# A hybrid decoder block on one core: values split within their own heads, quarter sums in two passes, convolution steps at uneven gaps

## The chip, the cores and the metric

The kernel runs on one core of one Trainium2 chip. The metric is the device time of one execution in microseconds, as the median of several runs. A core has TensorE (PE in the profile, PEld for its weight loads), VectorE (DVE), ScalarE (ACT), GpSimd (POOL) and SyncE (SP), each with its own queue of instructions that it works through in order; they wait for each other through semaphores. In this kernel nearly all DMAs are issued by SP.

## What is computed

One decoder layer on 1024 tokens of width 1024, in float32:

```python
h = rms_norm(x, g_pre_mix);  z = h @ w_in
q, k, v, glu_in, z_ga, z_gc = split(z)
y_attn = dilated_attention_mixer(q, k, v, rel_bias_table, w_attn_out)
y_conv = conformer_conv_mixer(glu_in, ...)   # GLU, causal depthwise conv of 31 taps, layer norm, silu, w_conv_out
merged = sigmoid(z_ga) * y_attn + sigmoid(z_gc) * y_conv
x = x + rms_norm(merged @ w_mix_out, g_post_mix)
x = x + rms_norm(swiglu_ffn(rms_norm(x, g_pre_ffn), w_ffn_in, w_ffn_out), g_post_ffn)
```

The attention has three groups of eight heads (width 64) with dilations 1, 4 and 16; in each group a query sees a band of 128 tokens' span (in its residue class) with a T5 bias. The three groups' outputs are merged with weights from their softmax denominators.

## The kernel before

Every float32 product is made of three products of reduced-precision halves (fp32r): a tensor is split into hi (a cast on ScalarE) and lo (a subtraction, on VectorE or GpSimd), and TensorE adds hi·hi, hi·lo and lo·hi. Most large products save one in eight by a Strassen-Winograd scheme on 2x2 quarters, `winograd` (L308): seven products of quarters in the order A11·B11, A12·B21, S2·T2, S1·T1, S3·T3, S4·B22, A22·T4. The S are sums of weight quarters (`quarters`, L183, in six steps c = 0 to 5, their lo halves and sums on the engine `wsplit`); the T are sums of the activation's quarters, made once per stage by `quarter_sums` (L341) and kept split.

The program's order is written by hand. `tick` (L113) is called after every k-tile, that is after three matmuls of 512 columns; it steps every generator in `gens` (a generator that yields n rests n ticks) and runs what is due: loads and weight splits, and one piece of weight splitting every `PIECE` ticks. `beat` (L131) is called after every matmul of the V products and of some later ones and steps the attention's generator at a rate of 0.33 or 0.66 per matmul. A product of `winograd` has four ticks, a pair of output tiles 28.

The stages:

1. `start` and the first GLU tiles, without the scheme, while the activation is normalised.
2. For GLU tile 3 (`FIRST` = 4) the quarter sums run as a generator: for each of four quarter tiles, T1 = b11 - b12, T2 = b22 - T1 (sign turned), T3 = b22 - b12 on `wsplit` (GpSimd here), T4, and their splits. `B.finish(qs)` (in `build`) issues what is left of them; then the convolution's generator joins.
3. 23 pairs with the scheme: 4 of GLU, 4 and 3 of gates, 12 of q and k (`qk_pair`, L735). An eviction adds the bank to a copied half on VectorE (L677, L682, L686, L710, L720; for q and k L761, L764, L771, L777, L783). Beside them `conv` (L595) does the depthwise convolution on VectorE: for each of 8 channel tiles, even and odd phases and their sum (L620), then 16 rounds of up to three multiply-adds into PSUM (L637, L632, L634), 47 steps, with a gap of 0 or 1 tick behind each (`CONV`), then the recombination (L642 to L647) and a running sum on GpSimd (L653).
4. The V products (`v`, L843) beside `conv_norm` (L1059) and then `attention` (L882). The attention has 12 pairs of heads of 8 steps. At step s: scores on TensorE (L937) and the bias with a running minimum on VectorE (L940) for block s; exponentials on ScalarE (L950) for s - 1; transposes (L973) and the split of the probabilities (L978 on ScalarE, L979 on VectorE) for s - 3; the product with V (L994, L996) for s - 4, reduced by VectorE (L1001). `stacks` (L790) loads q, k and the bias of the next pair at the present pair's second step and has GpSimd copy q to the other 64 partitions (L806, L807). `values` (L820) loads V at the fifth step, `value_parts` (L834) splits it at the seventh and eighth: a cast on ScalarE (L839), a subtraction on GpSimd (L840). The attention starts when `conv_norm` is done. In the third group `others` (L811) loads the two other groups' outputs and statistics, and `merge` (L1010) combines the three: small operations on the statistics (L1018 to L1025), three products with weights (L1029, the first on GpSimd), two sums (L1031, L1033) and transposes (L1040 to L1044).
5. The last gate tiles and the convolution's output projection, beside the attention's rest (`conv_split`, L1051, L1052; evictions L1348); the attention's output projection; the mix projection with its norm (L1409).
6. The FFN: two plain tile pairs, quarter sums again, 20 tiles with the scheme, and the output projection in seven products over 11 weight pairs (L1673).

Activations that are made early and used late go through DRAM (`d_u`, `d_conv`, `d_qk`, `d_v`, `d_att`, `d_st`). SBUF has 44 slots of 128 x 1024 ("b" in the profile) and 13 halves ("c"). PSUM has 8 banks, divided anew for some stages by `banks`; a division starts with the tag that is asked for first.

## Time and profile before

| | |
|---|---|
| median of 3 runs | 1788.83 us (1788.06 to 1788.92) |
| the profiled execution's own time | 1787.76 us |
| its span, first to last instruction | 1786.0 us |
| TensorE busy | 1725.8 us (97%), mean granted clock 0.986 |
| VectorE busy | 1251.7 us (70%) |
| ScalarE busy | 790.9 us (44%) |
| GpSimd busy | 505.8 us (28%) |
| moved by DMA | 274.94 MB, mean 154 GB/s |

A profile is of one execution. Times in it are us from the first instruction. A row of the table of waits reads: engine, tile and line that waited, the engine and line that it waited for, us in total, times, longest. A row by stretches reads: the stretch, its length, and for PE, PEld, DVE, ACT and POOL the busy us with the number of instructions in brackets; then the granted clock of TensorE, the DMA engines' busy share and GB/s. A row of groups reads: line, engine, operation, output and inputs by tile name, shape, count, then busy us and the mean in ns, then the idle time before and its causes. In a timeline a row has start, duration and the instruction, and in brackets the idle time before it and what ended it. A busy PE includes matmuls at a halved clock.

### The profile page before, as it was taken

To read this page: it belongs to the slowest core of one execution; us is meant where nothing else is said; L and a number is where in the kernel's file an instruction comes from. 1 tells how busy PE (TensorE), PEld (TensorE's weight loads), DVE (VectorE), ACT (ScalarE), POOL (GpSimd) and SP (SyncE) were. 2 spreads that over 40 slices of the span, in tenths; PEclk is the share of its full clock that TensorE was granted. 3 is DMA by queue.
4 is the path that set the end of the run, shared out by engine and by line. 5 is a ranking of instruction groups with operands and counts; after the bars stand their busy time and mean duration, and the time that the engine had idled before them with its cause. 6 is when DMAs were issued, how large, how long until landed. Compare 5 with 4: busy or idle time off the path is not lost.

```text
span 1786.0 us, 24511 instructions
## 1 busy us (share of the span) xinstructions
PE 1725.8 (97%) x8698; PEld 1462.3 (82%) x8698; DVE 1251.7 (70%) x2198; ACT 790.9 (44%) x1549; POOL 505.8 (28%) x357
## 2 busy tenths in 40 slices
PE   8989999999999989999898999999999999999998
PEld 6768888887777989998687888888888888878886
DVE  6899867899996546555676475586566565567686
ACT  6344344334433456556553145653333333353453
POOL 0067777877773223332320040040000000000000
PEclk9999999999999989999889999999999999999999
DMA  4333334556667576667753753203223223395234
GB/s 159 140 118 123 119 118 147 154 165 174 186 165 224 161 215 181 190 186 232 264 182 104 261 193 107 100 36 123 89 89 140 90 89 124 130 333 170 95 134 148
DMA packets 185783, 274.94 MB, mean 154 GB/s; under 512 B 56113, under 2 KB 107948, under 8 KB 185660
## 3 DMA queue, kind: packets, MB, share of 16 engines
q1 hardware_dynamic: 185020, 272.74, 47.6%
q8 instruction: 68, 1.11, 0.3%
q10 hardware_dynamic: 576, 0.56, 0.1%
q14 instruction: 55, 0.45, 0.1%
q0 software_dynamic: 64, 0.07, 0.0%
HBM read 183.76 MB, written 94.28 MB: 156 GB/s over the span
## 4 chain that ended last, share of the span: by engine, by line
PE 64%; DVE 5%; DMA 3%; ACT 2%; issue 1%; POOL 0%; SPq 0%; DVEq 0%; ACTq 0%; POOLq 0%
PE p L1673 12%; PE p L305 8%; PE p L303 8%; PE p L304 8%; PE p L1409 5%; PE p L291 3%; PE p L289 3%; PE p L287 3%; PE p L865 3%; PE p L867 3%; PE p L863 2%; PE p L937 2%; PE p L973 1%; PE p L996 1%; DMA b<-dv 1%
## 5 line engine op out<-in xcount | busy, mean ns | idle before, releaser
L303 PE MATMUL p<-b,b 128*128 128x512 f32 x1204 | 471.1, 391 | 14.0 <-DVE c L777 7.3
L305 PE MATMUL p<-b,b 128*128 128x512 f32 x1204 | 470.1, 390 | 0.4 <-POOL b L180 0.4
L304 PE MATMUL p<-b,b 128*128 128x512 f32 x1204 | 470.0, 390 | 0.0
L303 PEld LDWEIGHTS p<-b,b 128*128 128x128 f32 x1204 | 226.9, 188 | 64.8 <-DVE c L777 9.2
L305 PEld LDWEIGHTS p<-b,b 128*128 128x128 f32 x1204 | 227.0, 189 | 48.9 <-POOL b L180 1.5
L304 PEld LDWEIGHTS p<-b,b 128*128 128x128 f32 x1204 | 226.9, 188 | 46.7
L179 ACT CAST b<-b 128x1024 fp32r<-128x1024 f32 x129 | 135.6, 1051 | 181.0 <-POOL b L200 71.0
L1673 PE MATMUL p<-b,b 128*128 128x512 f32 x924 | 209.7, 389 | 1.5 <-DVE c L1582 1.5
L180 POOL TENSOR_TENSOR b<-b,b 128x1024 fp32r<-128x1024 f32 x72 | 175.6, 2438 | 115.7 <-ACT b L179 99.7
L1673 PEld LDWEIGHTS p<-b,b 128*128 128x128 f32 x924 | 173.3, 188 | 37.9 <-DVE c L1582 1.9
L637 DVE SCALAR_TENSOR_TENSOR p<-b,par,p 128x511 f32<-128x511 f32 (+14 forms) x232 | 163.6, 738 | 0.0
L180 DVE TENSOR_TENSOR b<-b,b 128x1024 fp32r<-128x1024 f32 x57 | 69.7, 1223 | 123.8 <-ACT b L179 123.8
L287 PE MATMUL p<-b,b 128*128 128x512 f32 x368 | 152.7, 415 | 0.8 <-DVE b L1348 0.8
L291 PE MATMUL p<-b,b 128*128 128x512 f32 x368 | 150.9, 410 | 0.0
L289 PE MATMUL p<-b,b 128*128 128x512 f32 x368 | 150.5, 409 | 0.0
L1052 DVE TENSOR_TENSOR b<-c,b 128x512 fp32r<-128x512 f32 x125 | 90.7, 736 | 39.7 <-ACT b L1051 39.4
L863 PE MATMUL p<-b,b 128*128 128x256 f32 x384 | 114.7, 299 | 2.2 <-DVE c L783 2.2
L865 PE MATMUL p<-b,b 128*128 128x256 f32 x384 | 114.7, 299 | 0.9 <-DVE b L173 0.9
L867 PE MATMUL p<-b,b 128*128 128x256 f32 x384 | 114.0, 297 | 0.0
L1051 ACT CAST b<-c 128x512 fp32r<-128x512 f32 x125 | 76.5, 618 | 56.0 <-DVE c L355 17.6
L979 DVE TENSOR_TENSOR c<-p,c 128x256 fp32r<-128x256 f32 (+1 forms) x96 | 52.3, 545 | 68.5 <-ACT c L978 60.2
L1409 PE MATMUL p<-b,b 128*128 128x512 f32 x384 | 88.9, 391 | 0.0
(222 smaller groups left out, 3042.6 us busy)
## 6 DMA issues: line engine op xcount, KB each, us to landing
b<-w_in SPq DMA_DIRECT2D x53, 512.0 KB, 4.8
b<-w_fi SPq DMA_DIRECT2D x44, 512.0 KB, 4.8
dk<-c SPq DMA_DIRECT2D x96, 128.0 KB, 2.5
dq<-c SPq DMA_DIRECT2D x96, 128.0 KB, 2.4
b<-dq SPq DMA_DIRECT2D x48, 256.0 KB, 7.1
b<-dk SPq DMA_DIRECT2D x24, 512.0 KB, 8.5
dqS<-c SPq DMA_DIRECT2D x44, 256.0 KB, 2.2
b<-w_fo SPq DMA_DIRECT2D x44, 256.0 KB, 5.4
```

The lines of the kernel that those rows point to most:

```text
L180: self.wsplit.tensor_tensor(lo, x, f(hi), op=OP.subtract)
L287: nc.tensor.matmul(ps, hi[:, s], a, start=kt == 0, stop=False)
L289: nc.tensor.matmul(ps, hi[:, s], b, start=False, stop=False)
L291: nc.tensor.matmul(ps, lo[:, s], a, start=False, stop=kt == nk - 1)
L303: nc.tensor.matmul(ps, hi[:, s], a, start=first and kt == 0, stop=False, skip_group_check=True)
L304: nc.tensor.matmul(ps, hi[:, s], b, start=False, stop=False, skip_group_check=True)
L305: nc.tensor.matmul(ps, lo[:, s], a, start=False, stop=kt == 3, skip_group_check=True)
L637: nc.vector.scalar_tensor_tensor(A[i][:, j:], src[i][:, :H - j], w[i], A[i][:, j:], op0=OP.mult, op1=OP.add)
L865: nc.tensor.matmul(o, a, lo[:, s], start=False, stop=False)
L867: nc.tensor.matmul(o, b, hi[:, s], start=False, stop=kt == KT - 1)
L1409: nc.tensor.matmul(banks[tt][nh], st, wt[:, nh * H:(nh + 1) * H], start=bool(kt == 0 and a), stop=bool(kt == KT - 1 and b))
L1673: nc.tensor.matmul(acc[t], x, y, start=first and e == 0, stop=last and e == 2, skip_group_check=True)
```

## The change

Five things are changed together.

- **Quarter sums.** `quarter_sums` makes T1 and T2 of all four tiles in a first pass, writing T2 over b11, and then hands out `self.T`; T3 and T4 follow in a second pass, in place over b22 and b21. In stage 2 `first_sums` only makes sure of the first pass; the rest runs on beside the first pair and is finished behind its fourth product (S1), where `summed` then sets `wsplit` to GpSimd and lets the convolution join. Until there `wsplit` is VectorE.
- **Convolution.** The gaps behind a step are (0, 1, 0, 0, 0, 1) in turn, and (1, 1, 0, 1) from q and k on, in place of (0, 1, 0, 1, 0, 1, 1). The sum of the phases moves to GpSimd and is issued at round 14 of the tile before.
- **Values and copies.** V is loaded as soon as the split of the present pair's is issued, and split at the third and fourth step of its own pair. The copies of q (`double`) are issued behind the sixth and seventh step of the pair before. The twelve empty steps behind a late load go.
- **Merge.** The statistics' loads are issued at the sixth step (`other_stats`), the outputs' loads one step later than before. The merge starts with two further ticks' rest, all three weighted products are on VectorE, and there are two more ticks before the transposes.
- **Banks.** For the V stage and for the output projection one bank of another tag is asked for first, so that the tags lie on other banks.

```diff
@@ Build
+    T, sums = None, None
+
+    def first_sums(self, e):
+        while self.T is None:
+            next(e[0])
+        self.sums = e
@@ winograd, behind S1's product
         nc.scalar.copy(v1, V)
+        if self.sums:
+            self.finish(self.sums)
+            self.sums = None
+            self.summed()
@@ quarter_sums
+        T["B11"], T["B21"], T["B22"] = blocks
...
+        for i in range(4):
+            b11, b12, b22 = B[0][i], B[1][i], B[1][i + 4]
+            t1 = self.half()
+            nc.vector.tensor_tensor(t1, b11, b12, op=OP.subtract)
+            nc.vector.scalar_tensor_tensor(b11, t1, -1.0, b22, op0=OP.mult, op1=OP.subtract)
+            keep("T1", t1)
+            yield 1
+            keep("T2", b11)
+            yield 3
+        self.T = T
         for i in range(4):
             b11, b12, b21, b22 = B[0][i], B[1][i], B[0][i + 4], B[1][i + 4]
-            t1, t2, t3 = self.half(), self.half(), self.half()
-            nc.vector.tensor_tensor(t1, b11, b12, op=OP.subtract)
-            nc.vector.scalar_tensor_tensor(t2, t1, -1.0, b22, op0=OP.mult, op1=OP.subtract)
-            if last is not None:
-                keep("T4", last)
-                last = None
-            self.wsplit.tensor_tensor(t3, b22, b12, op=OP.subtract)
-            keep("T1", t1)
+            self.wsplit.tensor_tensor(b22, b22, b12, op=OP.subtract)
+            nc.vector.scalar_tensor_tensor(b21, b11, -1.0, b21, op0=OP.mult, op1=OP.subtract)
+            yield 0
+            keep("T3", b22)
             yield 1
-            nc.vector.scalar_tensor_tensor(t1, t2, -1.0, b21, op0=OP.mult, op1=OP.subtract)
-            keep("T2", t2)
-            keep("T3", t3)
...
-            yield 4
+            keep("T4", b21)
+            yield 0
@@ conv
+        def phases(u):
+            x = u.rearrange("p (m e) -> p e m", e=2)
+            s = self.half()
+            nc.gpsimd.tensor_tensor(s, x[:, 0], x[:, 1], op=OP.add)
+            return x[:, 0], x[:, 1], s
...
-            nc.vector.tensor_tensor(s, x[:, 0], x[:, 1], op=OP.add)
+            src = src or phases(nxt)
...
+                if j == 14 and nxt is not None:
+                    ahead = phases(nxt)
...
-    cg, CONV = 0, (0, 1, 0, 1, 0, 1, 1)
+    cg, CONV = 0, (0, 1, 0, 0, 0, 1)
@@ attention
+                if x is None and nxt and there():
                     x = self.values(*nxt[:2])
...
                 if u == 8:
-                    while after in self.gens or nxt[0] * 2 + nxt[1] // 2 >= self.vn:
+                    while after in self.gens or x is None:
+                        if x is None and there():
+                            x = self.values(*nxt[:2])
                         yield 0
...
                 self.att_s(a, cur, V, u)
                 u += 1
+                if u in (3, 4):
+                    V.append(self.value_parts(x, u - 3))
+                    if u == 4:
+                        x = None
+                if u == 6 and cur[0] == 2:
+                    self.other_stats(cur)
+                if u in (6, 7) and nxt:
+                    self.double(nxt, u - 6)
...
-            if s % 8 == 1 and s > 64 and live[s - 2]["p"][0] == 2:
-                self.others(live[s - 2]["p"])
+            if s % 8 == 2 and s > 64 and live[s - 3]["p"][0] == 2:
+                self.others(live[s - 3]["p"])
@@ merge
+        yield 2
...
-            (nc.gpsimd if g == 0 else nc.vector).tensor_tensor(y, y, a, op=OP.mult)
+            nc.vector.tensor_tensor(y, y, a, op=OP.mult)
...
-        yield 3
+        yield 5
@@ build
-    B.wsplit = nc.gpsimd
...
-    B.finish(qs)
-    conv = B.bg(conv)
+    B.first_sums(qs)
+
+    def beside():
+        B.wsplit = nc.gpsimd
+        B.bg(conv)
+
+    B.summed = beside
...
+    B.CONV = (1, 1, 0, 1)
     for g in range(3):
         for hp in range(4):
             B.qk_pair(g, hp, qkj[g, hp])
...
     B.banks(g=2, s=2, t=2, o=2)
+    B.bank("s")
...
-    B.banks(g=8)
+    B.banks(y=4, x=4)
+    B.bank("y")
```

More of the change, by code (lines that the diff above doesn't have):

```diff
@@ L639, in conv @@
                     yield self.conv_gap
-            u = x = src = None
+            src = ahead
             o = self.slot()
@@ L885, in attention, with there @@
         order = [(g, hp) for g in range(3) for hp in range(4)]
-        nxt, cur, u, x, V = self.stacks(*order.pop(0)), None, 8, None, []
+        nxt, cur, u, x, V = self.stacks(*order.pop(0)), None, 8, None, None
+        def there():
+            return nxt[0] * 2 + nxt[1] // 2 < self.vn
         while s < total + self.LP:
             if s < total:
-                if x is None and nxt and u > 3 and nxt[0] * 2 + nxt[1] // 2 < self.vn:
+                if x is None and nxt and there():
                     x = self.values(*nxt[:2])
-                elif u in (6, 7) and x is not None:
-                    V.append(self.value_parts(x, u - 6))
@@ L902, in attention @@
-                    now, cur, u, nxt, x, V = V, nxt, 0, None, None, []
+                    if cur is None:
+                        self.double(nxt, 0)
+                        self.double(nxt, 1)
+                    V, cur, u, nxt = [], nxt, 0, None
                 live[s] = a = {}
-                self.att_s(a, cur, now, u)
+                self.att_s(a, cur, V, u)
                 u += 1
+                if u in (3, 4):
+                    V.append(self.value_parts(x, u - 3))
+                    if u == 4:
+                        x = None
@@ L1296, in build @@
     B.PIECE = 6
-    B.finish(conv)
+    for _ in conv:
+        pass
+    B.gens = [e for e in B.gens if e[0] is not conv]
     assert bl not in B.gens
     B.banks(g=2, s=2, t=2, o=2)
+    B.bank("s")
     B.OT, B.merges = {}, []
@@ L1660, in half0 @@
             yield from out_norm(0, t, (1, c), 1)
-    X, Y = [B.bank() for _ in range(4)], None
+    X, Y = [B.bank("x") for _ in range(4)], None
     for i in range(7):
         if i == 1 or i == 3:
-            Y = [B.bank() for _ in range(4)]
+            Y = [B.bank("y") for _ in range(4)]
         acc = Y if i in (1, 3, 4) else X
```

48 lines of the change are left out of this document (18 added, 30 removed).

## The prediction

> **What bounds the kernel now.** I read the page first, then the table of waits of PE, then a table by stretches for the clock, and last the timelines and groups of the places that the waits name.
>
> ```profile
> span 1786.0 us, 24511 instructions
> PE 1725.8 (97%) x8698; PEld 1462.3 (82%) x8698; DVE 1251.7 (70%) x2198; ACT 790.9 (44%) x1549; POOL 505.8 (28%) x357
> ```
>
> TensorE is the bound nearly everywhere. Its work does not change, so a change can only win its idle time, and the time that it runs at a lower clock. The idle time by cause:
>
> ```profile
> PE p L973 <- ACT c L950: 8.0, 1, 8.0
> PE p L303 <- DVE c L777: 7.3, 4, 3.6
> PE p L994 <- ACT c L978: 7.1, 5, 3.5
> PE p L303 <- ACT c L317: 5.0, 2, 4.3
> PE p L1040 <- issue: 3.1, 1, 3.1
> PE p L994 <- DVE b L1001: 2.6, 2, 2.1
> PE p L996 <- DVE c L979: 2.5, 5, 0.7
> PE p L863 <- DVE c L783: 2.2, 1, 2.2
> PE p L1673 <- DVE c L1582: 1.5, 1, 1.5
> PE p L303 <- ACT c L322: 1.1, 1, 1.1
> PE p L303 <- DVE c L682: 0.6, 1, 0.6
> ```
>
> (Who waited, for whom: us in total, times, longest.) The second loss is the clock. The table by stretches shows PE busy and the granted clock (the figure behind POOL's bracket) where it was halved:
>
> ```profile
> 109.00:118.00 9.00, 5.81 (x16) 4.64 (x17) 9.00 (x10) 3.26 (x5) 7.15 (x4) 0.62 0.17 58
> 499.00:503.00 4.00, 4.00 (x12) 3.10 (x12) 4.00 (x7) 1.50 (x3) 3.14 (x2) 0.57 0.64 137
> 563.50:568.00 4.50, 4.07 (x21) 4.07 (x22) 1.11 (x3) 0.00 (x0) 0.00 (x0) 0.62 0.89 189
> 642.50:652.80 10.30, 6.22 (x29) 6.02 (x30) 2.82 (x8) 8.62 (x26) 6.17 (x8) 0.50 0.87 220
> 857.50:864.50 7.00, 7.00 (x25) 6.04 (x25) 5.96 (x18) 5.57 (x19) 1.28 (x1) 0.51 0.74 289
> 878.00:885.00 7.00, 5.65 (x19) 4.79 (x20) 2.63 (x10) 2.06 (x8) 0.00 (x0) 0.51 0.47 186
> 891.50:895.50 4.00, 4.00 (x17) 3.37 (x17) 4.00 (x15) 2.14 (x9) 3.94 (x3) 0.57 0.02 6
> 915.50:922.50 7.00, 6.94 (x24) 5.99 (x25) 7.00 (x18) 3.28 (x13) 0.94 (x1) 0.51 0.92 308
> ```
>
> Busy time times the missing share of the clock is the loss: 2.2, 1.7, 1.5, 3.1, 3.4, 2.8, 1.7 and 3.4 us, 19.8 us together. Each stretch lies on or right behind one of the waits above, so a wait that goes takes its clock loss along. The trace drops the clock behind short waits too (561: 2.2 us). The Trainium skill, "TensorE: Matmul & The Clock Gate", Part 1, states one idle window of about 3.4 us as the condition; by it only the waits of 3.5 us and more would have cost clock, and the trace shows more than that. I go by the rows.
>
> **The change part by part.** The sum is made against the profiled execution's 1787.76 us (span 1786.0 and 1.8 around it); the median of the runs, 1788.83, is 1.07 higher.
>
> **Quarter sums (before the first pair).** Their DVE steps lie among GpSimd's; the last row is PE's first use of T2, in S2's product:
>
> ```profile
> 83.68 0.69 DVE L355 TENSOR_TENSOR c<-b 128x512 f32<-128x512 f32 x1
> 99.80 2.76 POOL L180 TENSOR_TENSOR b<-b,b 128x1024 fp32r<-128x1024 f32 x1 [7.63 <-DVE b L1052]
> 100.22 2.88 DVE L355 TENSOR_TENSOR c<-b 128x512 f32<-128x512 f32 x1
> 112.19 0.79 PE L303 MATMUL p<-b,b 128*128 128x512 f32 x1 [4.29 <-ACT c L317]
> ```
>
> The same subtraction takes 0.69 us alone and 2.88 beside GpSimd. The Trainium skill, "SBUF — State Buffer", section "SBUF: two separate sides", says that a GpSimd instruction and a DVE one with two SBUF inputs exclude each other for a whole instruction; the rows agree. After the change GpSimd has no part here until the first pair's fourth product. The first pass (T1, T2) is 4 x (2 sums and 2 subtractions of a split) at 0.69, 11 us of DVE from 83.7, with a weight split or two between: done near 97. S2's product, whose wait begins at 107.9 (112.19 - 4.29), finds T2. What is late next: the second pass, 11 us, with the first pair's weight sums and splits now on DVE (three 1024-wide at some 1.2 and five at 0.69: 7 us, of which about 4 before 97), and two evictions of 0.7: 97 + 11 + 3 + 1.4, or 112.4 to 113.5. T3 and S3 are wanted 8 ticks behind T2, a tick being three matmuls of 0.226 us (below): 107.9 + 5.4 = 113.3. I leave 0.6 us. Gain: 4.3 + 0.6 + 2.2 - 0.6 = 6.5. The convolution starts 16 ticks later. At the FFN the same function has 40 ticks where 32 are; the rest is issued in one go, with 16 ticks until T3 is wanted. Nothing, up to 2 us if ScalarE's casts wait there for GpSimd's T3.
>
> **Convolution.** A block has 47 steps, one to a tick and a gap. Before, gaps of 4/7 on average: 47 x 1.57 + 4 = 77.9 ticks. After: 66.7 ticks (gap 1/3) until q and k, 86.3 (gap 3/4) behind. The 11 gated pairs have 308 ticks, less 16; 4.4 blocks fit, and the other 3.6 take 312, so it ends at tick 620 of 644, where it ended before (623). DVE's load, before:
>
> ```profile
> 122.00:179.00 57.00, 56.40 (x249) 46.40 (x248) 53.87 (x72) 21.96 (x33) 42.78 (x24) 1.00 0.35 117
> 200.00:317.00 117.00, 117.00 (x518) 96.89 (x517) 86.20 (x132) 46.62 (x71) 89.24 (x53) 1.00 0.36 128
> 340.00:559.00 219.00, 209.47 (x907) 170.36 (x906) 208.78 (x264) 87.55 (x128) 162.28 (x90) 0.99 0.65 173
> L637 DVE SCALAR_TENSOR_TENSOR p<-b,par,p 128x507 f32<-128x507 f32 (+14 forms) x107 | 75.6, 736 | 0.0
> L637 DVE SCALAR_TENSOR_TENSOR p<-c,pairs,p 128x507 f32<-128x507 f32 (+13 forms) x52 | 38.3, 737 | 0.0
> L620 DVE TENSOR_TENSOR c<-b 128x512 f32<-128x512 f32 x3 | 7.6, 2539 | 0.0
> ```
>
> The first row is the GLU pairs, the second the gates (117 us for 518 matmuls: 0.226 each, 0.68 a tick), the third q and k; the groups are of the third. There DVE has 208.78 us of work in the 208 us that PE would need without its 11 us of loss: it is the bound, evictions (L777) queue behind steps, and PE waits. After: steps 114 us x (77.9/86.3) saves 11, L620 goes to GpSimd and saves 7.6: 190 of 208, 91%. The gates rise by a sixth of 75: 98 of 117. The GLU pairs rise by 6 and lose 1.7: 58 of 57, that is 1.4 us late over three pairs, within the four ticks (2.7 us) that lie between an eviction and the product that needs its bank. L620 on GpSimd: between 0.69 (DVE alone) and 2.8 us, eight of them; I take 1.4, as L840 below has for 512 on GpSimd; it is hidden, issued two of sixteen rounds ahead. If that cover is gone, DVE waits 1.4 us a block.
> The Trainium skill's rule above speaks against this part, since GpSimd then locks DVE out: by it up to 8 x 1.4 = 11 us of DVE, spread over stages with room. L620's own 2539 ns say that DVE pays that already. Today's loss: L777 7.3, L322 1.1, the shorter L317 0.7, 1.7 of clock: 10.8. I leave 2.5 for bursts at a block's end: gain 8.3.
>
> **Banks.** The empty allocations turn the order, so that the first V unit and the first output products take a bank that the last pair's last eviction (L783, L1582) does not read. Gain 2.2 + 1.5 of clock, less 1.0 for the V weights' last split, which today ends after that wait; and 1.5 - 0.2 at the output. Together 4.0.
>
> **Values.** The casts of V for the next pair (L839) stand in ScalarE's queue before the exponentials of the present one, and wait for a load issued two steps ahead:
>
> ```profile
> ACT b L839 <- DMA b<-dv: 23.4, 8, 8.1
> ACT b L1051 <- PE p L937: 5.2, 1, 5.2
> 643.58 1.14 ACT L839 CAST b<-b 128x512 fp32r<-128x512 f32 x2 [8.10 <-DMA b<-dv]
> 855.32 0.62 ACT L839 CAST b<-b 128x512 fp32r<-128x512 f32 x1 [3.10 <-DMA b<-dv]
> DVE mrg L1018 <- DMA stat<-dst: 4.6, 1, 4.6
> L807 POOL CAST b<-b 64x512 fp32r<-64x512 f32 x48 | 33.7, 702 | 10.5 <-DMA b<-dq 6.9 <-PE p L996 1.3 <-DMA b<-dk 0.7
> L840 POOL TENSOR_TENSOR b<-b,b 128x512 fp32r<-128x512 f32 x24 | 33.0, 1376 | 91.4 <-ACT b L839 83.2 <-PE p L867 4.9 <-PE p L937 3.3
> L937 PE MATMUL p<-b,b x384: 220/280/415, 635.1 to 938.7; 128*128 128x128 f32 x104, 128*128 128x256 f32 x88
> 826.00:980.00 154.00, 138.24 (x755) 116.33 (x754) 105.01 (x305) 77.15 (x238) 37.86 (x39) 0.92 0.59 188
> ```
>
> After the change the load is issued at the same step but used seven steps on. 96 steps between 635 and 939 are 3.2 us each: 22 us, where 6.4 and waits of up to 8.1 stand today. The first pair's load goes out as soon as its V tiles are stored, no longer behind the convolution's norm, and the twelve empty steps before its use go. Start: today 8.0 + 3.1 of clock. Left are the exponentials' table load and V's first cast, some 2 us. Gain 9.1. The copies of q are issued later in GpSimd's order, but an engine runs its queue as its inputs land: the first pair's still run long before 635, and a later pair's eight copies (8 x 0.7 = 5.6 us) have two steps of 3.2 and, for their second half, four steps more.
>
> **Statistics and merges.** The statistics are loaded three steps earlier and the merge begins three ticks later, so DVE's wait at L1018 (4.6) goes, and with it ScalarE's. SP issues the two small loads earlier and the two large ones a step later, behind the same stacks and past V's load; the merge's products come six ticks behind its start and cover that. The product with w[0] moves to DVE: some 1.2 us more of it, less what GpSimd's pass cost beside it. O's tiles come free sooner, which can only ease the slots. From 780 to 960 the waits for L978, L1001 and L979 are 12.2 us and the clock's last four stretches 11.3: 23.5. Not all of it is dv or statistics (L1001's 2.1 us goes back to L1051, a cast that waited 5.2 us for a slot), so I take two thirds, 16. The last merge: two ticks more before its transposes, 1.4 of L1040's 3.1.
>
> **Sum.** 6.5 + 8.3 + 4.0 + 9.1 + 16 + 1.4 = 45.3; 1787.8 - 45.3 = 1742.5, and 1.07 for the median: 1743.5, say **1743 us**.
>
> **The rivals.**
> - **Everything goes**: all of the named losses, 7.1 + 10.8 + 5.2 + 11.1 + 23.5 + 3.1 = 60.8: 1728. For it: each has one cause. Against: q and k at 91% of DVE, slots still full.
> - **The attention's waits only move**: SP and ScalarE wait for slots, and the DMA engines at up to 0.92 in these stretches; then 4 of the 16 come: 1755.
> - **DVE stays the bound**: with GpSimd busy 162 of 219 us and given L620, the two-input steps stretch further, and the GLU pairs fall 4 us behind. None of the 8.3 comes, and 4 go: 1756. With the one before, 1768. Speaks against it: 18 us of DVE removed in q and k.
> - **Slower**: V's split now stands in its own pair. It is issued behind the third step and needed at the end of the fifth, two steps or 6.4 us on; cast and subtraction take 0.6 + 1.4. If copies that wait for their load hold GpSimd, every pair waits: 12 us for each us beyond the margin of 4.4. From 8.2 us of delay on (3.8 x 12 = 45) the kernel is slower; at 9 us it is at 1743 + 55 = 1798. Against it: in 91.4 us of idle before L840 no copy's load appears as cause.
> - **It doesn't do what it says**: the load could still go out late, if slots are short; that is the second rival.
>
> **How the numbers follow.** Forecast 0.51; everything goes 0.13; waits move 0.17; DVE 0.10, both 0.03; slower 0.05; nothing (0.2%, 3.6 us, about what a measurement here can tell) 0.01. Faster 0.94, same 0.01, slower 0.05. The range from 1726 (the first rival, with a little) to 1765 leaves out the double rival and those behind it, about 1 in 10.
>
> **What would show it.** No wait of PE for L317 near 107 and a clock of 1.00 there; no L777 among PE's waits, and DVE under 0.95 in q and k; L863 and L1673 without waits; L839 without a wait for dv; a clock of 1.00 around 640 and above 0.97 from 826 to 980. The prediction is wrong if L994 waits for L840, if L682 or L690 stand among the causes near 140 to 180, or if waits of SP for slots grow.

## The result and the profile after

The kernel before takes 1788.85 us in the runs beside it, the changed kernel 1763.38 us (median of four, 1759.38 to 1768.65): 0.986 times the time, 95% interval 0.9834 to 0.9887. The forecast was 1743; of its gain of 45 us, 25 came. The profiled execution took 1763.24 us, with a span of 1761.4.

The head of the page of the changed kernel, span and busy times by engine:

```profile
span 1761.4 us, 24497 instructions
...
PE 1714.6 (97%) x8698; PEld 1454.6 (83%) x8698; DVE 1245.9 (71%) x2207; ACT 792.3 (45%) x1549; POOL 478.5 (27%) x348
```

Its table of waits of PE (who waited, for whom: us in total, times, longest):

```profile
PE p L311 <- ACT c L325: 9.3, 2, 8.1
PE p L524 <- ACT b L504: 7.7, 1, 7.7
PE p L1026 <- DVE c L1009: 4.7, 5, 2.4
PE p L313 <- POOL b L188: 3.9, 3, 2.3
PE p L967 <- DMA b<-dk: 2.5, 1, 2.5
PE p L1024 <- DVE b L1031: 1.8, 1, 1.8
PE p L1024 <- issue: 1.8, 1, 1.8
PE p L1003 <- DVE b L1077: 1.7, 1, 1.7
...
PE p L1073 <- issue: 0.8, 1, 0.8
PE p L311 <- DVE c L792: 0.7, 2, 0.5
```

Gone are the 8.0 us at the attention's start and the two waits for banks; those for the q/k eviction (L777, now L792) are down from 7.3 us to 0.7. But the first line is L317's wait of before (the copy `x1`), and it has grown from 4.3 to 8.1 us. The stretches with a halved clock, in the table by stretches (the clock stands behind POOL's bracket):

```profile
111.70:122.00 10.30, 5.46 (x13) 4.35 (x14) 9.88 (x16) 4.33 (x7) 0.00 (x0) 0.50 0.48 175
859.20:869.50 10.30, 6.11 (x20) 5.17 (x21) 9.56 (x28) 5.04 (x18) 0.72 (x2) 0.50 1.05 331
879.70:883.10 3.40, 3.40 (x13) 2.81 (x13) 2.24 (x11) 1.11 (x5) 3.10 (x6) 0.50 0.68 185
490.60:494.00 3.40, 3.40 (x9) 2.65 (x9) 3.40 (x6) 1.03 (x1) 1.46 (x1) 0.50 1.09 319
```

Half of the busy time is lost: 2.7 + 3.1 + 1.7 + 1.7 = 9.2 us, where 19.8 were.

Where the 24.6 us of span came from, by stages that PE's timeline bounds (each begins with the first matmul of its kind; "the last scores" are the attention's last product for scores, L937, now L967):

| stage | before | after | difference | forecast |
|---|---|---|---|---|
| up to the first gated pair | 102.2 | 102.9 | +0.7 | 0 |
| the first pair | 26.8 | 30.0 | +3.2 | -6.5 |
| second pair to the first q/k product | 190.4 | 190.6 | +0.2 | 0 |
| q/k, to the first V product | 244.5 | 236.4 | -8.1 | -8.3 and -2.7 |
| V, to the last scores | 374.8 | 353.6 | -21.2 | -9.1 and -16 |
| from there to the end | 847.3 | 848.0 | +0.8 | -1.4 and -1.3 |

So q/k gave most of what was expected of it, the stage from V to the last scores somewhat less, and the first pair lost 3.2 us where it was to win 6.5.

The last two rows hold different work before and after. The attention is stepped 0.33 times per matmul, so its twelve empty steps were 36 matmuls; without them it runs that far ahead of the other products, and some of these fall behind the last scores. By stretches, from the last scores to the first matmul of the mix projection, before and after:

```profile
938.70:1046.30 107.60, 102.44 (x471) 84.07 (x471) 67.00 (x110) 31.28 (x64) 11.10 (x11) 1.00 0.54 193
```

```profile
913.40:1022.40 109.00, 106.74 (x492) 87.69 (x492) 69.34 (x114) 31.72 (x62) 7.89 (x9) 1.00 0.53 190
```

That is 21 matmuls and 4.3 us of PE's work more, which the stage ahead has less (2619 matmuls for 2640). With this shift taken out, an estimate from these counts, the stage from V to the last scores won some 17 us, and the end some 3.5.

### The profile page after: what moved, and what is told of

The parts are those of the page before. It is cut to its first block, busy times and chain, and to the rows that moved or that the text cites. A ratio compares the mean times of both kernels' runs of the same rounds, so it can differ in the third digit from the quotient of the medians.

```text
span 1761.4 us, 24497 instructions
## 1 busy us (share of the span) xinstructions
PE 1714.6 (97%) x8698; PEld 1454.6 (83%) x8698; DVE 1245.9 (71%) x2207; ACT 792.3 (45%) x1549; POOL 478.5 (27%) x348
## 4 chain that ended last, share of the span: by engine, by line
PE 84%; DVE 5%; DMA 4%; ACT 3%; issue 2%; POOL 1%; SPq 1%; DVEq 0%; ACTq 0%; POOLq 0%
PE p L311 13%; PE p L312 13%; PE p L313 13%; PE p L1718 12%; PE p L1452 5%; PE p L299 4%; PE p L295 4%; PE p L297 4%; PE p L885 2%; PE p L883 2%; PE p L887 2%; PE p L524 2%; PE p L967 2%; DMA b<-w_in 1%; PE p L1003 1%
## 5 line engine op out<-in xcount | busy, mean ns | idle before, releaser
L312 PE MATMUL p<-b,b 128*128 128x512 f32 x1204 | 470.1, 390 | 0.0
L312 PEld LDWEIGHTS p<-b,b 128*128 128x128 f32 x1204 | 227.1, 189 | 47.3
L187 ACT CAST b<-b 128x1024 fp32r<-128x1024 f32 x129 | 135.6, 1051 | 199.2 <-POOL b L208 73.4
L188 POOL TENSOR_TENSOR b<-b,b 128x1024 fp32r<-128x1024 f32 x69 | 167.3, 2425 | 129.9 <-ACT b L187 117.6
L188 DVE TENSOR_TENSOR b<-b,b 128x1024 fp32r<-128x1024 f32 x60 | 73.4, 1223 | 127.3 <-ACT b L187 127.3
L1086 DVE TENSOR_TENSOR b<-c,b 128x512 fp32r<-128x512 f32 x101 | 71.3, 706 | 40.5 <-ACT b L1085 40.1
L1086 DVE TENSOR_TENSOR b<-b,b 128x512 fp32r<-128x512 f32 x117 | 84.7, 726 | 17.3 <-ACT b L1085 15.3
L1085 ACT CAST b<-b 128x512 fp32r<-128x512 f32 x117 | 72.1, 619 | 44.5 <-PE p L1718 13.1
```

The lines of the kernel that those rows point to most:

```text
L188: self.wsplit.tensor_tensor(lo, x, f(hi), op=OP.subtract)
L312: nc.tensor.matmul(ps, hi[:, s], b, start=False, stop=False, skip_group_check=True)
L1086: nc.vector.tensor_tensor(s[:, 512:512 + n], src, f(s[:, :n]), op=OP.subtract)
```

## The experiments

All times of runs below are medians, and ratios go by the kernel before in the same job. The kernel before spread from 1780.7 to 1797.2 over these jobs, so the stages of the profiled runs carry most of the argument. How well a stage repeats can be read from q/k: ten profiles of kernels that have the change's convolution and steps of q/k show 232.8 to 236.4 us, 234.3 on average. "Third group" is the attention's last four pairs, from their first scores to the last; seven profiles in which the change's third group runs as it is (the change, the four runs s_, c_dve and c_old) show 98.6 to 102.4 us, so a difference of 3 us there says little. Where a line was put in, the line numbers behind it are a few higher than in the changed kernel.

| run | time | ratio (95%) | first pair | q/k | V to last scores | third group |
|---|---|---|---|---|---|---|
| the change | 1763.4 | 0.986 (0.9834 to 0.9887) | 30.0 | 236.4 | 353.6 | 100.1 |
| s_old | 1757.1 | 0.9837 (0.9815 to 0.9858) | 27.5 | 234.3 | 355.2 | 102.2 |
| s_hold | 1754.7 | 0.9822 (0.9799 to 0.9846) | 25.0 | 233.5 | 352.2 | 99.8 |
| s_t3 | 1766.5 | 0.9884 (0.9861 to 0.9906) | 31.7 | 235.2 | 352.1 | 99.0 |
| s_slot | 1758.6 | 0.9841 (0.9817 to 0.9865) | 27.2 | 233.8 | 354.4 | 98.6 |
| c_dve | 1759.9 | 0.9857 (0.9838 to 0.9877) | 24.9 | 235.2 | 355.2 | 101.7 |
| c_old | 1770.2 | 0.9919 (0.9897 to 0.9941) | 30.2 | 237.5 | 356.9 | 102.4 |
| v_old | 1772.1 | 0.9928 (0.9909 to 0.9948) | 29.7 | 233.8 | 367.9 | 98.3 |
| a_cs | 1757.7 | 0.9846 (0.9827 to 0.9865) | 23.5 | 233.0 | 357.0 | 104.0 |
| a_lo | 1753.6 | 0.9788 (0.976 to 0.9815) | 23.5 | 235.2 | 352.2 | 98.8 |
| a_q | 1781.0 | 0.9951 (0.9932 to 0.9971) | 23.5 | 234.9 | 378.3 | 112.4 |
| b_banks | 1786.6 | 0.9985 (0.9967 to 1.0003) | 26.8 | 246.2 | 381.3 | 107.0 |
| a_half | 1742.8 | 0.9751 (0.9721 to 0.9781) | 23.5 | 232.8 | 342.3 | 90.0 |

### The first pair: whose queue holds the copy x1

ScalarE's timeline of the changed kernel (start, us, instruction; in brackets its idle time and what ended it) carries the theory:

```profile
102.82 1.05 ACT L187 CAST b<-b 128x1024 fp32r<-128x1024 f32 x1 [3.88 <-PE p L297]
106.47 0.62 ACT L1085 CAST b<-b 128x512 fp32r<-128x512 f32 x1 [2.60 <-DVE b L377]
108.26 0.62 ACT L1085 CAST b<-b 128x512 fp32r<-128x512 f32 x1 [1.17 <-PE p L312]
110.28 1.18 ACT L1085 CAST b<-b 128x512 fp32r<-128x512 f32 x2 [1.40 <-DVE b L377]
114.73 1.28 ACT L1085 CAST b<-b 128x512 fp32r<-128x512 f32 x2 [3.27 <-DVE b L377]
115.91 0.58 ACT L325 COPY c<-p 128x512 f32<-128x512 f32 x1
```

L325 copies the first product out of its bank; S2's product may add to that bank only behind it. The copy itself waits for nothing. It stands behind six casts of the second pass. Before four of these ScalarE is idle, 8.4 us together: three times the row names VectorE's T3 (L377), once a matmul (L312). **Theory Q**: this order costs the 8.1 us. Rivals: VectorE simply has too much to do there (D), or the slot that L187 waits 3.88 us for delays it all (S).

**s_old** puts the quarter sums alone back: one pass, T3's subtraction and the weights on GpSimd, all done before the pair.

```diff
-    B.first_sums(qs)
...
+    B.finish(qs)
+    B.bg(conv)
```

> The changed kernel, with the quarter sums alone put back as they were (one pass, T3's subtraction and the weights on GpSimd, all finished before the first pair). Theory Q (order of ScalarE's queue: the copy x1 stands behind the second pass's casts, so the wait at the first pair is 8.1 us where it was 4.3): the wait returns to about 4.3, the first pairs end some 3 to 4 us sooner than in the changed kernel, and the whole is 1759 to 1760 where the changed kernel's profiled run has 1763.2. The prediction on record: this part was worth 6.5 us, so without it the time is about 1770.

PE's waits from 96 to 135:

```profile
PE p L311 <- ACT c L325: 4.3, 1, 4.3
PE p L311 <- DVE c L699: 1.3, 1, 1.3
```

The first pair is 2.5 us shorter than in the changed kernel, and the whole 1757.1; a ratio up to 0.9858 leaves no room for 1770. The part did not win 6.5 us; it cost 2.5 us by this run, 3.2 against the kernel before.

**s_hold** keeps the two passes and issues the second only once the copy is in ScalarE's queue.

```diff
         self.T = T
+        while self.held:
+            yield 0
         for i in range(4):
...
         nc.scalar.copy(x1, X)
+        self.held = False
```

> The changed kernel, with the second pass (T3, T4) held back until ScalarE has been given the copy x1 of the first pair's first product. Theory Q: the wait for x1 (8.1 us) and the halved clock behind it go; T3's last split then lands near 118 where S3's product wants it near 115, so 2 to 4 us of wait for T3 (line 1088 or so, VectorE) take its place; time 1754 to 1758. Rival D (VectorE has too much to do there, whatever the order): the wait for T3 is as long as the old one, 7 to 8 us; time 1762 to 1764. Rival S (a slot held by GLU tile 3's weights keeps ScalarE's L187 waiting 3.9 us, and everything behind is late by that): the L187 wait stays, and T3's wait is 4 us or more.

ScalarE's copy, from its timeline, and then PE's waits from 96 to 135:

```profile
104.86 0.59 ACT L325 COPY c<-p 128x512 f32<-128x512 f32 x1 [1.89 <-PE p L313]
```

```profile
PE p L311 <- ACT b L1088: 1.4, 2, 1.2
PE p L311 <- ACT c L331: 1.0, 1, 1.0
PE p L312 <- DVE b L1089: 0.5, 2, 0.2
```

The copy now follows TensorE's product at once, some eleven us sooner. The splits of the second pass are late by 1.4 + 0.5 us and the next copy by 1.0: the 1.9 us lie just under the 2 to 4 that Q gave, and far from D's 7 to 8. L187 still waits 3.89 us, and the splits are late by half of what S gave. A halved clock there did not go altogether (last section). The pair takes 25.0 us for 30.0, and the whole 1754.7.

**s_t3** goes one step on, with all T3 before all T4.

```diff
             keep("T3", b22)
             yield 1
+        for i in range(4):
+            b11, b21 = B[0][i], B[0][i + 4]
+            nc.vector.scalar_tensor_tensor(b21, b11, -1.0, b21, op0=OP.mult, op1=OP.subtract)
             keep("T4", b21)
-            yield 0
+            yield 1
```

> As the one that holds the second pass back, and in it all four T3 first, then all four T4. Theory Q: T3's last split lands some 4 us sooner, the wait for T3 is under 1 us, T4's splits come in time (its product is issued eight ticks, 5.4 us, behind T3's); time 1752 to 1756. Rival D: the wait only moves on to T4, 4 us or more; 1758 to 1762.

A miss, of both. PE's waits from 96 to 135, and two rows of ScalarE's timeline:

```profile
PE p L311 <- ACT c L331: 4.4, 1, 4.4
PE p L311 <- DVE c L701: 4.0, 1, 4.0
```

```profile
116.36 0.62 ACT L1089 CAST b<-b 128x512 fp32r<-128x512 f32 x1 [1.50 <-DVE b L380]
116.88 0.58 ACT L331 COPY c<-p 128x512 f32<-128x512 f32 x1
```

The four T3 now come at two ticks each, and the cast that waits for the last of them is given to ScalarE before `x2` (L331), S2's copy. So the next copy stands behind a cast: the same mechanism, one product later, and 31.7 us for the pair. Of the 11.8 us by which this run is slower than s_hold, 6.7 are this pair and 3.7 the part behind the attention, where PE waits 3.5 us (1.4 in s_hold) for the copy `x1` of the FFN's first pair, whose sums the same function makes. The order in which a queue is given its entries decides, not how early T3 begins.

**s_slot** has 45 large slots and 11 half ones (44 and 13).

```diff
-NSLOT = 44
-NHALF = 13
+NSLOT = 45
+NHALF = 11
```

> The changed kernel with 45 large slots where it has 44, and 11 half ones where it has 13 (the memory for one). Rival S: ScalarE's wait at L187 near 102 (3.9 us) goes, VectorE's idle 3.5 us with it, and the wait for x1 falls from 8.1 to about 4.5; some 4 to 5 us with its clock, 1758 to 1760. Theory Q alone: the wait at L187 may go, but the casts of the second pass still stand ahead of x1, which waits 7 us or more. In both cases fewer half tiles may cost waits elsewhere, which the landmarks up to the second pair leave out.

From ScalarE's timeline:

```profile
99.20 1.06 ACT L187 CAST b<-b 128x1024 fp32r<-128x1024 f32 x1 [0.91 <-DVE b L208]
...
113.82 0.58 ACT L325 COPY c<-p 128x512 f32<-128x512 f32 x1
```

ScalarE's wait is 0.91 us for 3.88, but VectorE now waits 3.17 us for the next slot, the one for the same split's low part. PE's wait for the copy, still behind its casts, is 6.0 us for 8.1, between what Q (7 or more) and S (4.5) gave, and the pair takes 27.2 us for 30.0. So the late slot has a share in the loss, 2.8 us here; the order alone, with the slot as late as before, was worth 5.0 (s_hold). One slot is too few to tell what slots cost in all.

### The convolution in q and k

**c_dve** is s_hold with the running sum of the blocks' outputs on VectorE. In the changed kernel GpSimd's timeline shows it ahead of the weight split that PE waits 2.3 us for:

```profile
485.53 2.41 POOL L667 TENSOR_TENSOR b<-b,b 128x1024 f32<-128x1024 f32 x1 [0.78 <-DVE b L661]
487.90 2.36 POOL L188 TENSOR_TENSOR b<-b,b 128x1024 fp32r<-128x1024 f32 x1
```

```diff
-                nc.gpsimd.tensor_tensor(self.csum, self.csum, o, op=OP.add)
+                nc.vector.tensor_tensor(self.csum, self.csum, o, op=OP.add)
```

> The kernel that holds the second pass back, and in it the convolution's running sum (one 128x1024 addition at the end of each block) on VectorE where it stood on GpSimd. Theory G (order of GpSimd's queue): the weight splits L188 that PE waits for stand behind that sum, 2.4 us of GpSimd each; PE's waits for L188 (3.9 us in the changed kernel, 3.0 with the second pass held back) go, and the clock's drop near 490 with them; from the first q/k product to the first V product 230 to 232 us, where the two runs have 236.4 and 233.5. Rival D (VectorE is still the bound in q and k): four more additions of 1.2 us there push the evictions, waits for the evictions' line (792 in the changed kernel) take their place, and the stage stays at 233 or more.

From PE's table of waits:

```profile
PE p L311 <- DVE c L795: 3.7, 3, 1.9
...
PE p L311 <- DVE c L738: 1.6, 2, 0.9
```

L188 has left the table, and evictions (L795, L738) have taken its place; the stage takes 235.2. D was right: either queue, GpSimd's or VectorE's, is late at a block's end.

**c_old** is the changed kernel with the convolution's part put back: L620 on VectorE at a block's start and the old gaps.

```diff
-            nc.gpsimd.tensor_tensor(s, x[:, 0], x[:, 1], op=OP.add)
+            nc.vector.tensor_tensor(s, x[:, 0], x[:, 1], op=OP.add)
...
-    cg, CONV = 0, (0, 1, 0, 0, 0, 1)
+    cg, CONV = 0, (0, 1, 0, 1, 0, 1, 1)
...
-    B.CONV = (1, 1, 0, 1)
```

> The changed kernel with the convolution's part alone put back: the pair sums on VectorE at a block's start, its steps with the old gaps (4/7 on average) from start to end. The prediction on record: this part was worth 8.3 us, nearly all in q and k, of which the changed kernel's stage shows a gain of 8.1 us together with the first bank's 2 to 3; so the stage from the first q/k product to the first V product grows from 236.4 to 241 to 243, PE's waits for the eviction of q/k (7.3 us in four, before) come back, and the time is 1767 to 1771. Rival (the gain there came from the banks and from GpSimd's other load, not from the spreading): the stage stays within 235 to 238 and the time at 1760 to 1765.

The q/k stage by stretches, in three fences: the kernel before, the changed one, and this one (PE, PEld and DVE busy, with counts, follow the length):

```profile
319.40:563.90 244.50, 232.76 (x1009) 189.31 (x1007) 230.32 (x294) 98.50 (x146) 180.59 (x99) 0.99 0.64 172
```

```profile
323.40:559.80 236.40, 231.82 (x1009) 189.79 (x1008) 210.25 (x266) 95.53 (x142) 183.62 (x101) 0.99 0.65 172
```

```profile
325.30:562.70 237.40, 230.83 (x1009) 188.33 (x1008) 225.93 (x301) 97.14 (x144) 178.01 (x98) 1.00 0.64 173
```

The stage is 3 us over the average of 234.3, not 8: in the rival's range, while the time, 1770.2, is in the first one's. VectorE is as loaded as before the change (226 of 237 us, 95%; before, 94%), and the stage is 7 us shorter than before all the same. PE's longest wait for an eviction in it is 2.6 us. By time, c_old loses 0.0059 of 1788 to the changed kernel, 10.5 us with an error of some 6; its stages show 1.1 us more in the gated pairs, 1 to 3 in q/k, 3.3 in V and the attention.

**b_banks** is the kernel before with the banks' edits alone.

```diff
+    B.bank("s")
...
-    B.banks(g=8)
+    B.banks(y=4, x=4)
+    B.bank("y")
```

> The kernel before, with the two edits of the banks alone. The prediction on record: PE's waits for L783 and L1582 go, 2.2 and 1.5 us with 1.5 of clock, less 1.0 and 0.2: 4.0 us, 1783 to 1785 against 1787 to 1788 in the same job. What it tells besides: the stage from the first q/k product to the first V product, 244.5 us before and 237.5 with the old convolution in the changed kernel. If the banks made that difference, it is 238 to 240 here; if the convolution's start 16 ticks later did (its blocks' ends then meet other steps of the pairs), it is 241 to 243 here, with the waits for L777 as before.

From PE's table of waits (the profiled run was its slowest, 1793.9; its median is 1786.6, 2.7 us less by the ratio, with an error of some 3):

```profile
PE p L303 <- DVE c L777: 7.8, 5, 3.6
...
PE p L865 <- DVE b L173: 1.6, 3, 0.7
```

The two waits for banks are gone, and at the first V product 0.7 us for V's last split stands in place of 2.2. But the stage is 246.2, above both ranges, with L777 as before, so the banks did not shorten q/k. The old gaps with the new quarter sums and banks gave 237.5 (c_old); the new gaps with the old sums gave 234.3 (s_old); old sums and old gaps gave 244.5 and 246.2. Either edit alone brings most of the gain. Common to both is that they move the convolution's blocks against the pairs: the sums start it 16 ticks later, the gaps change its pace. Before, the two longest of the four waits for L777 (3.6 and 2.7 us) fell where a block's end, L620 (2.89 and 2.43 us) and the next block's first steps stood in VectorE's queue ahead of the eviction. That the shift is the cause is inferred from these four; a kernel with the shift alone was not run.

### The values

**v_old** splits V in the last steps of the pair before, issues q's copies with the loads, and has the twelve empty steps.

```diff
-                if u in (3, 4):
-                    V.append(self.value_parts(x, u - 3))
...
+                elif u in (6, 7) and x is not None:
+                    V.append(self.value_parts(x, u - 6))
```

> The changed kernel with the values' part alone put back: V's tiles split in the last steps of the pair before, q's copies issued with the loads, the twelve empty steps ahead of the first pair. The prediction on record: the wait of 8 us near 643 and the clock behind it come back, and most of the 16 of the attention's later waits; from the first V product to the end of the attention 375 us (375 before, 353.6 in the changed kernel), the time 1775 to 1785. Rival (only the start is worth something; the later waits belong to loads, slots and the merges): 361 to 366 from V to the end of the attention, 1770 to 1776.

From PE's table of waits:

```profile
PE p L1018 <- ACT c L1002: 8.8, 4, 6.3
PE p L997 <- ACT c L974: 7.7, 1, 7.7
```

The wait at the start is back at 7.7 us, and others with it: 367.9 us for 353.6, between what the first forecast and the rival gave; the time, 1772.1, is in the rival's range. Of the 14.3 us some 3 are work that this kernel, with its empty steps, does ahead of the last scores and the changed one behind them; from the first V product to the kernel's end the difference is 11.2 us. Most of it is at the start. By stretches, from the first scores to those of the third pair, in the kernel before, the changed one and this one:

```profile
635.10:687.90 52.80, 44.83 (x362) 44.42 (x361) 26.74 (x92) 30.36 (x91) 17.86 (x22) 0.90 0.70 192
```

```profile
625.30:668.60 43.30, 42.14 (x362) 41.89 (x361) 26.96 (x93) 29.13 (x89) 15.08 (x20) 1.00 0.87 252
```

```profile
626.70:678.80 52.10, 44.37 (x363) 43.96 (x362) 26.61 (x92) 30.66 (x91) 17.91 (x22) 0.90 0.71 194
```

The work is the same, and the change wins 9.5 us of it, this kernel 0.7. From the third pair to the third group it is 146.6, 144.7 and 147.0 us, and in the third group this kernel, at 98.3, is no slower than the others. So the rival was nearly right: the values' part is worth its start and some 2 us behind it.

### The third group

It fell only from 104.2 to 100.1 us, and that by the clock (0.93 for 0.89): PE's idle time in it grew from 9.8 to 12.3 us.

**a_cs** is s_hold with the convolution's outputs split 16 ticks later behind their first loads.

```diff
         x = [load(i) for i in range(5)]
-        yield 8
+        yield 24
```

> The kernel that holds the second pass back, and in it the convolution's outputs split sixteen ticks later behind their loads (24 where 8 are). Theory A (order of ScalarE's queue again: a cast that waits 5.5 us for its load at 854 stands ahead of the exponentials, and PE waits behind them): that wait goes, the clock stays at 1.00 from 855 to 870, and the attention's third group (from its start at 813 in the changed kernel to its end at 913, 100.1 us) takes 95 to 97 us; time 1749 to 1752. Rival M (the DMA engines are full, 0.97 to 1.05 from 800 to 870, whatever the order): another load is late instead, of k, q or the other groups' outputs, and the group takes 99 to 101 us; time 1753 to 1756.

The group took 104.0 us, outside both ranges. The edit didn't do what it was made for: ScalarE's waits for these loads came to 7.0 us in three, the longest 3.4, where s_hold has 6.2 in two, the longest 4.6; and PE now waited 3.9 us for VectorE in another place. So this run says nothing on Theory A; the next one does.

**a_lo** leaves out eleven of the sixteen loads and keeps every split (the first five tiles are read again).

```diff
-            self.cop[i // 8].append(self.split(x.pop(0), H))
-            if i < 11:
-                x.append(load(i + 5))
+            x.append(x.pop(0))
+            self.cop[i // 8].append(self.split(x[-1], H))
```

> The kernel that holds the second pass back, with eleven of the sixteen loads of the convolution's output left out of the attention's third group (its splits read the first five tiles again and again, so the convolution's branch is wrong): 2.9 MB less of the 20 MB that move from 800 to 870, at 291 GB/s some 10 us of full DMA engines, and no split that waits for a late load. Theory M (the DMA engines, full at 0.97 to 1.05 from 800 to 870, set the third group's waits): the waits behind loads there go or shrink, the clock stays up, and the group takes 91 to 96 us where it took 99.8. Rival O (the order of ScalarE's and VectorE's queues and the last pairs' merges set it, not the DMA engines): 98 to 100 us.

98.8 us for 99.8, with no wait of ScalarE for these loads in the group and the DMA engines at 0.75 for 0.83: neither their load nor a late load of these sets the group, and Theory A falls with M. Rival O holds so far.

**a_q** issues the same loads from ScalarE's queue.

```diff
-            nc.sync.dma_start(x, self.d_act[b][:, hf * H:(hf + 1) * H])
+            nc.scalar.dma_start(x, self.d_act[b][:, hf * H:(hf + 1) * H])
```

> The kernel that holds the second pass back, with the same sixteen loads issued from ScalarE's queue where SP's issued them, so that they don't stand behind loads that wait on SP for a free slot. Theory M (the DMA engines are full): no change worth naming, 99 to 101 us for the third group, 1753 to 1757. Rival P (SP's order: the two loads of the other groups' outputs wait there for slots until 851, and the convolution's loads behind them): ScalarE's wait for the load at 854 (5.5 us) goes, and the group takes 95 to 97 us; 1749 to 1752. Either way ScalarE spends some time on issuing sixteen loads.

Both theories missed what it would do. ScalarE's waits from 790 to 905:

```profile
ACT b L180 <- DMA c<-dact: 13.3, 1, 13.3
...
ACT b L862 <- DMA b<-dgc: 9.4, 1, 9.4
```

ScalarE idled 13.3 us while the first five loads stood in its queue (the last of them went out at 799), with its next casts and the exponentials behind them, and 9.4 us behind another load near 858. The first stop falls ahead of the third group: from V to the group it is 265.9 us for 252.4 in s_hold, and the group took 112.4. A load that may have to wait belongs on a queue where nobody waits behind it.

**a_half** leaves out the splits of the second half of the tokens: eight loads, casts and subtractions, and the eight slots they fill.

```diff
-            self.cop[i // 8].append(self.split(x.pop(0), H))
-            if i < 11:
+            self.cop[i // 8].append(self.split(x.pop(0), H) if i < 8 else self.cop[0][i - 8])
+            if i < 3:
```

> The kernel that holds the second pass back, with the splits of the convolution's second half of tokens left out of the attention's third group: eight loads, casts and subtractions, and the eight large slots that they take near 850 (the first half's are used twice, so half of the convolution's branch is wrong). Theory N (slots: near 861 and 866 ScalarE's casts of V wait 3.4 and 3.2 us for a slot that a merge or a unit's weights still hold, and the exponentials behind them): both waits go, the wait for a late load near 848 too, and the third group takes 90 to 95 us where it took 99.8. Rival R (those waits are not what PE waits for; the group is set by the chain of the last pairs' steps from TensorE through ScalarE and VectorE and back, and by the clock behind each stop): 97 to 100 us.

s_hold's two casts of V, in ScalarE's timeline, and the group by stretches, first in s_hold and then here:

```profile
861.47 0.62 ACT L862 CAST b<-b 128x512 fp32r<-128x512 f32 x1 [3.43 <-DVE b L1065]
866.33 0.62 ACT L862 CAST b<-b 128x512 fp32r<-128x512 f32 x1 [3.21 <-PE p L297]
```

```profile
803.30:903.10 99.80, 89.32 (x526) 76.89 (x525) 73.85 (x240) 57.34 (x196) 25.86 (x32) 0.91 0.83 241
```

```profile
802.00:892.00 90.00, 85.18 (x527) 74.25 (x525) 68.82 (x231) 53.59 (x188) 26.32 (x32) 0.96 0.83 243
```

The two waits are gone, and the group takes 90.0 us, with as many matmuls and the DMA engines as full (0.83). Of the 9.8 us, 5.7 are idle time of PE and the rest is its clock. In a_lo, which leaves out more loads but keeps the splits and their slots, both waits stand (3.9 and 3.2 us), and it won 1.0; so most of the other 8.8 us belong to the slots or to the work of the eight splits themselves (eight casts of 0.62 us, eight subtractions). The casts that wait are of V, in their own pair as the change has it, and what they wait for is a slot. How the 8.8 divide between slots and the splits' work was not settled.

**s_hold beats both kernels**: 0.9822 of the time before, where the changed kernel has 0.986. The intervals overlap; what shows the gain is the first pair, 25.0 us in it and 23.5 to 24.9 in the five other kernels with its edit (s_t3 aside), for 29.7 to 30.2 in the three profiles with the change's own sums and slots.

## Why the prediction came out as it did

The time lay in the range, 20 us above the forecast, and the sign was right. That the range held is in part luck: its upper end is 1.6 us away, one of the four runs lies beyond it, and the largest miss, the first pair, is one that no rival had. By spans 24.6 of the 45.3 us came. Of what is missing, 9.7 us are the first pair, 2.9 q/k, 7.3 all that follows from V to the end, and 0.9 stretches that were to stay as they were. By its steps:

- **Quarter sums: failed.** The step is "S2's product, whose wait begins at 107.9 ..., finds T2", from which followed "Gain: ... 6.5". T2 was there (VectorE's first pass ended at 100.4). But the row that the step rested on names `<-ACT c L317`, the copy x1, and not T2: it was read as a wait for an operand, when it was one for a bank, through a queue. The second pass then put six casts ahead of that copy, most of whose waiting was for VectorE. It cost 3.2 us. s_old and s_hold show it from both sides; s_slot adds that a late slot made it worse.
- **Convolution: size right, reason wrong.** VectorE's work in q/k fell as worked out (230.3 to 210.3 us), L620 on GpSimd took 1339 ns on average in that stage for the 1.4 taken, and L777's waits fell from 7.3 to 0.7 us. The stage gained 8.1 of 11.0 (with the first bank); this profile is the slowest of the ten, whose average gives 10.2. But "it is the bound" was not so: c_old, at 95% of VectorE, lost only some 3 us there. What the four profiles point to instead are a few meetings of a block's end with an eviction, which either edit moved away; that is inferred, not shown. On the rule that speaks against the part: the Trainium skill, "SBUF — State Buffer", section "SBUF: two separate sides", lets GpSimd's L620 lock out a VectorE instruction with two inputs in SBUF. By that rule VectorE's busy time should have kept some of what L620 gave; the rows show it 20.1 us lower, 18.6 having been worked out. A cost can hide in this: the subtraction of the q/k split (L761, now L776), with both inputs in SBUF, took 1679 ns on average for 1421, while the steps with an operand in PSUM took 738 for 737. Whether L620 did that, or other meetings with GpSimd's weight splits, was not tested.
- **Banks: 4.0 forecast.** Both waits went. b_banks is 2.7 us faster, with an interval that takes in both nothing and 4.0, so the size is not shown.
- **Values and the start: right.** The stall and its clock went as said, 9.5 us for the 9.1 forecast (first scores to the third pair's). The 5.8 us by which the first scores come sooner behind V (65.4 for 71.2) are for the most part the twelve empty steps, that is work which now comes later.
- **Statistics, merges and the attention's body: mis-sized.** This is the term "two thirds, 16". Some 6 came: 1.9 from the third pair to the third group, and 4.1 in the third group. There the second rival ruled ("the waits only move", with slots named as its cause): the waits for L978 went, waits of PE for k, for VectorE (L1009, L1031, L1077) and of ScalarE for slots and late loads stand in their place, and two stretches of halved clock. Which of these the slots cause is open; a_half narrows it to slots or the splits' work.
- **The last merge: right, and hidden.** L1040's 3.1 us became 0.8 (L1073). The stretch from the last scores to the mix grew from 107.6 to 109.0 us all the same, because it holds 4.3 us more of PE's work; PE's idle time in it fell from 5.2 to 2.3 us.

Of the signs that the prediction named, these came: L863 and L1673 without waits, the cast of V without a wait for dv, VectorE at 0.89 in q/k, a clock of 1.00 at 640, and L777 down to 0.7 us. These did not: the wait near 107 stayed, and the clock from 826 to 980 is 0.96, not above 0.97. Of the signs of being wrong none came: PE waits neither for V's subtraction (L840, now L860) nor for an eviction between 140 and 180, and SP's waits in the third group did not grow (65 us for 76).

## What to carry to other kernels

A wait names its releaser: look there at what stands ahead of the releaser in its own queue before deciding that the operand is late. When work is split in two and made to run beside the consumer, issue each copy that frees a bank ahead of any cast that must wait for another engine. A high busy share of an engine off the critical path is no proof that it is the bound: put the load back with the timing changed, and see. Before stages are compared, count the matmuls in each: work that has moved from one to the next looks like time won.

## What the chip showed that was not expected

The clock fell behind waits that are each short. In s_hold no wait of PE between 96 and 135 is over 1.2 us, 2.9 us together, and yet, by stretches:

```profile
117.00:120.00 3.00, 1.58 (x6) 0.86 (x5) 2.86 (x6) 2.12 (x3) 0.00 (x0) 1.00 0.00 0
120.00:122.00 2.00, 2.00 (x6) 1.56 (x5) 2.00 (x4) 0.00 (x0) 1.97 (x1) 0.50 0.00 0
```

The Trainium skill, "TensorE: Matmul & The Clock Gate", Part 1, states one idle window of about 3.4 us as the condition; these rows do not agree: waits that add up to 2.9 us within ten were followed by a halved clock. Nor are several waits needed. In the same trace PE has one wait between 880 and 900, of 1.39 us, and this is what follows it:

```profile
888.00:891.40 3.40, 2.01 (x13) 1.62 (x13) 3.40 (x9) 2.14 (x7) 1.28 (x1) 1.00 0.09 34
891.40:894.80 3.40, 3.40 (x12) 2.88 (x12) 3.40 (x11) 1.26 (x5) 0.00 (x0) 0.50 0.32 118
```

In a_half a wait of 1.37 us at 878.5, alone, left the clock at 1.00. So a short wait can cost clock or not; what decides it was not settled here.
